# One chain for the first attention's modulation products, with loads a step ahead and a third raw slot; the samples' gate table loaded at the end of the attention's loop

## The chip, the cores and the metric

One core of a Trainium2 chip. The metric is device time in microseconds (us) of one execution of the whole program, the median of several runs. The engines: PE (TensorE, matmuls; PEld is its weight load), DVE (VectorE), ACT (ScalarE), POOL (GpSimd), and SP (SyncE), which issues every DMA of this kernel in one order, fixed when the program is built. Each engine, too, has one fixed order of instructions; an instruction that waits holds up all behind it on its engine.

## What is computed

One inference step of a two-layer encoder over 1024 prompt rows and 8 samples of 16 rows (1152 rows, width 1024). A layer is an attention and a convolutional MLP, each of this form:

```python
ada = (sc @ w_ada[l] + b_ada[l])[:, None, :]          # sc = silu(c), 9 rows: prompt + 8 samples
sh_m, sc_m, g_m, sh_f, sc_f, g_f = jnp.split(ada, 6, axis=-1)
h = x * (1 + sc_m) + sh_m
...
x = layer_norm(DEEPNORM_ALPHA * x + (1 + g_m) * mix, ln_g[l, 0], ln_b[l, 0])
```

Layer 0 attends to its own 64-row chunk and two before it, with 16 query heads, 4 key heads, a relative bias and sinks; layer 1 attends over 8 chunks back with keys and values of its own. The MLP is gelu-gated with a causal convolution of width 3.

## The kernel before

All arithmetic is float32 grade: every operand is split into a high and a low part (`split`: ACT casts the high part, L183, then DVE or POOL subtracts it, L194), and each product is three matmuls, low part of the weights first. A weight block of 512 KB is loaded into a raw slot of the ring `ws` (two slots), split into a slot of the ring `wring`, and then used (`wload`, L198).

The program opens with the first third of layer 0's modulation and the keys (`opening`), then `tables` and `attention(0)`. In the attention: keys' second half (L300), values (`vproj`, L326: nine tiles of 128 rows, the last three being 5, 6 and 7), then query block 0 (`qload(0)`, `qblock`, L313: 72 matmuls), whose weights go to the `wring` slot `w0r`. Then a loop over 64 pairs: scores (L558, L561), softmax (L525, L529), transposes (L587), values (L609), sums (L635), normalisation (L644, L647), the later query blocks, and from pair 24 on the 16 sample items (L701, L727, L736, L749). Values and keys go to DRAM and come back in another layout (kH, vH). On their way the eviction tiles are staged in X2 (named x2r) and, for what goes to the outputs, in six short tiles of the buffer F, at columns 9120, 9504, 10400, 11520, 11904 and 12288. Tile 7 of the values uses the one at 11520 and leaves from there to out_va (L388).

In the loop `self.step(BGA)` runs background work at 0.6 steps a pair: two generators `ada(1, 4)` and `ada(2, 4)`, the modulation groups 1 and 2. A step of `ada` loads one 512 KB block of w_ada into a raw slot (L232) and multiplies it by the conditioning rows (L240, 4 matmuls of 32 rows each, in the trace 8); after 16 steps one step loads the four bias pieces (L255) and adds them (L259), writes the gate table gd (L263, L265), and one transposes the result (L268). Groups 1 and 2 hold the gates of the attention and the scales and shifts of the MLP. While they run, score tiles have four PSUM banks; afterwards five.

Behind the loop, `out_proj` lays out F anew (`ln_region`), loads the prompt's gate row and the samples' gate table (`ln_gates`, L971 and L972) and the norm's rows behind the last normalisation's DMA, and then multiplies nine tiles of 128 rows (L326), the samples' tile first; L1122 multiplies a tile by its gates.

The order of the instructions is not that of the code: a scheduler places each by a model of the time in which it becomes ready, keeps what the data demand, and fixes the order of each engine. Matmuls of one modulation step are kept together by priorities (L232 ff.).

Of the kernel before, what the change touches and what calls it, by code (L numbers as in the profile page):

```python
# [10 lines left out]
F32 = mybir.dt.float32  # L11
# [4 lines left out]
D = 1024  # L16
# [89 lines left out]
class Trunk:  # L106
# [116 lines left out]
    def ada(self, gi, bank, ring=None):  # L223

        nc = self.nc
        ring = ring or self.ws
        ps = self.bank(bank)
        lead = [None] * 4
        for k in range(8):
            for hf in range(2):  # L230
                w = ring.next()
                nc.sync.dma_start(w, self.I["adaw"][gi, k, hf])  # L232
                for j in range(4):
                    with ExitStack() as es:
                        if lead[j] is not None:
                            es.enter_context(self.tc.issue_after(lead[j]))
                        if j:
                            es.enter_context(self.tc.high_priority())
                            es.enter_context(self.tc.issue_after(first))
                        mm = nc.tensor.matmul(  # L240
                            ps[32 * j : 32 * j + 32, hf * 256 : hf * 256 + 256],
                            self.cT[:, k * 32 : k * 32 + 32],
                            w[:, j * 256 : j * 256 + 256],
                            start=k == 0 and hf == 0,
                            stop=k == 7 and hf == 1,
                            tile_position=(0, 32 * j),
                            skip_group_check=True,
                        )
                    first = mm.ins if j == 0 else first
                    lead[j] = lead[j] or mm.ins  # L250
                yield
        row = ring.next()
        bsrc = self.I["adab"][gi : gi + 1, :]
        for j in range(4):
            nc.sync.dma_start(  # L255
                row[32 * j : 32 * j + 32, 512:1024].rearrange("p (h x) -> p h x", h=2),
                bass.AP(bsrc.tensor, bsrc.offset + j * 256, [[0, 32], [1024, 2], [1, 256]]),
            )
        nc.vector.tensor_add(row[:, 0:512], ps, row[:, 512:1024])  # L259
# [6 lines left out]
        yield  # L266
        for i in range(4):
            nc.tensor.transpose(ps[:, i * 128 : i * 128 + 128], row[:, i * 128 : i * 128 + 128], self.ident)  # L268
# [124 lines left out]
    def attention(self, l, wk):  # L393
        nc, I = self.nc, self.I
# [41 lines left out]
        assert fa.o <= self.NF, fa.o  # L436
        sbk = Ring(list(SB[l]))
        tbk = Ring(TB[l])
        obk = Ring(OB[l])
# [505 lines left out]
    def ln_region(self):  # L945
        fa = Arena(self.F)
        x = fa.take(2048)
        self.xring = Ring([x[:, i * 1024 : i * 1024 + 1024] for i in range(2)])
        y = Arena(x)
        self.yg = y.ring(2, 384)  # L950
        self.at = y.ring(2, 384)
        for k in ("hf", "xr", "tmp"):
            setattr(self, k, fa.take(1024))
        self.E = fa.take(704)
        self.cw = fa.take(176)
        self.uo = [fa.take(198) for _ in range(2)]
# [4 lines left out]
        self.zt = fa.take(1024)  # L961
        assert fa.o <= self.NF, fa.o

    def ln_consts(self, l, i):
        self.ln_gates(l, i)
        self.ln_rows(l, i)

    def ln_gates(self, l, i):
# [3 lines left out]
        nc.sync.dma_start(self.gateS, bass.AP(g.tensor, g.offset + D, [[D, 8], [0, 16], [1, D]]))  # L972

    def ln_rows(self, l, i):
        nc = self.nc
# [118 lines left out]
    def out_proj(self, l, xsrc, xdst, aff):  # L1094
        nc, I, H = self.nc, self.I, self.H
        w = [self.wo[i] if i in self.wo else self.woload(l, i) for i in range(8)]
        w0, w1 = w[0:4], w[4:8]
        self.wring = Ring(self.wslots[3:4] + self.wslots[0:3])
        self.ln_region()
        with self.tc.issue_after(self.lastdma):  # L1100
            self.ln_consts(l, 0)
        mb = Ring([0, 1, 2, 3])
        tb = Ring([4, 5, 6, 7])
        hfr = Ring([self.hf, self.zt])
        order = (8, 0, 1, 2, 3, 4, 5, 6, 7)
        acc = {}

        def half(t, hf):
            acc[t, hf] = self.bank(mb.next())
            self.mmX(acc[t, hf], t * 128, (w0, w1)[hf], 2, 512)  # L1110

        for t in order[:2]:
            half(t, 0)
        for t in order:
            if t not in order[:2]:
                half(t, 0)
            half(t, 1)
            x = self.residual(t, xsrc)
            gate = self.gateP if t < 8 else self.gateS
            for hf in range(2):  # L1120
                cs = slice(hf * 512, hf * 512 + 512)
                nc.vector.tensor_mul(self.tmp[:, cs], acc[t, hf], gate[:, cs])  # L1122
            nc.vector.scalar_tensor_tensor(x, x, ALPHA, self.tmp, op0=ALU.mult, op1=ALU.add)
            self.norm_tail(t, x, xdst, aff, False, tb, "a", "pv", Ring([self.xr]), hfr, hdst=self.hD)
# [812 lines left out]
    def build(self):  # L1937
        nc, I, O = self.nc, self.I, self.O
        self.bgrate = 0
        wk = self.opening()  # L1940
        self.bg = [self.ada(1, 4), self.ada(2, 4)]
        self.tables()
        self.attention(0, wk)
        self.drain()
        aff = self.affine(0, (3, 4), 0)
        self.out_proj(0, I["xrow"], self.xd[0], aff)
        self.ffn(0, self.xd[0], self.xd[1], lambda: self.affine(3, (6, 7), 1))
        self.attention(1, None)
        self.out_proj(1, self.xd[1], self.xd[2], self.affine(5, (11, 12), 2))
        self.ffn(1, self.xd[2], O["y"], lambda: None)  # L1950
# [131 lines left out]
```

## Time and profile before

| | us |
|---|---|
| median of 3 runs (2744.03 to 2745.9) | 2744.65 |
| profiled execution, whole | 2745.36 |
| profiled execution, span from first to last instruction | 2743.6 |
| mean granted clock of PE | 0.990 of full speed |
| first attention with opening and values | 0 to about 380 |
| output projection of layer 0 | about 380 to 460 |

The profile's page gives busy times of the engines over the span; further views list groups of instructions, waits (who waited for whom), the instructions in order of time, and busy times and clock by stretches. Times in them count from the span's start. The granted clock is the share of PE's full clock that its throttle let through.

### The profile page before, as it was taken

To read this page: it belongs to the slowest core of one execution; us is meant where nothing else is said; L and a number is where in the kernel's file an instruction comes from. 1 tells how busy PE (TensorE), PEld (TensorE's weight loads), DVE (VectorE), ACT (ScalarE), POOL (GpSimd) and SP (SyncE) were. 2 spreads that over 40 slices of the span, in tenths; PEclk is the share of its full clock that TensorE was granted. 3 is DMA by queue.
4 is the path that set the end of the run, shared out by engine and by line. 5 is a ranking of instruction groups with operands and counts; after the bars stand their busy time and mean duration, and the time that the engine had idled before them with its cause. 6 is when DMAs were issued, how large, how long until landed. Compare 5 with 4: busy or idle time off the path is not lost.

```text
span 2743.6 us, 47063 instructions
## 1 busy us (share of the span) xinstructions
PE 2639.7 (96%) x17266; PEld 2339.8 (85%) x17266; DVE 1936.4 (71%) x3840; ACT 1350.6 (49%) x2777; POOL 1069.0 (39%) x771
## 2 busy tenths in 40 slices
PE   7999889999999999999999999989989999999997
PEld 5997768989999998888898888867889999998886
DVE  4376768786676675767854667776888877778668
ACT  3475734443333344443536666573444455546553
POOL 2132523444443457665220121242367666652101
PEclk9999999999999999999999999999999999999999
DMA  8756534744444447666758546774444433349673
GB/s 298 234 155 199 152 104 169 239 155 140 140 150 148 153 144 231 238 207 203 261 196 264 146 136 182 207 232 134 160 149 171 150 134 138 123 140 301 222 236 123
DMA packets 229527, 498.27 MB, mean 182 GB/s; under 512 B 37456, under 2 KB 99232, under 8 KB 229296
## 3 DMA queue, kind: packets, MB, share of 16 engines
q1 hardware_dynamic: 229296, 495.27, 55.6%
q8 instruction: 136, 2.23, 0.3%
q14 instruction: 95, 0.78, 0.1%
HBM read 378.15 MB, written 126.47 MB: 184 GB/s over the span
## 4 chain that ended last, share of the span: by engine, by line
PE 38%; DVE 6%; DMA 3%; issue 1%; ACT 1%; POOL 1%; SPq 0%; DVEq 0%; POOLq 0%; ACTq 0%
PE PS L1237 14%; PE PS L1627 9%; PE PS L326 5%; PE PS L313 4%; PE PS L609 2%; PE PS L587 2%; DVE wl L194 1%; PE PS L558 1%; PE PS L561 1%; DVE F L525 1%; PE PS L736 1%; DVE xa L194 0%; DVE F L1197 0%; DMA F<-in_cvB_dram 0%; DVE PS L1286 0%
## 5 line engine op out<-in xcount | busy, mean ns | idle before, releaser
L1237 PE MATMUL PS<-H,wh 128*128 128x256 f32 (+1 forms) x2304 | 352.4, 294 | 0.0
L1237 PEld LDWEIGHTS PS<-H,wh 128*128 128x128 f32 x2304 | 319.8, 188 | 0.0
L1197 DVE TENSOR_TENSOR F<-PS,F 128x256 f32<-128x256 f32 (+1 forms) x446 | 196.9, 451 | 165.1 <-PE PS L1237 155.7
L183 ACT CAST wh<-F 128x512 fp32r<-128x512 f32 (+3 forms) x221 | 135.5, 625 | 196.8 <-PE PS L1237 96.2
L194 DVE TENSOR_TENSOR wl<-F,wh 128x512 fp32r<-128x512 f32 (+2 forms) x205 | 197.1, 972 | 44.1 <-ACT wh L183 40.6
L1237 PE MATMUL PS<-H,wl 128*128 128x320 f32 (+1 forms) x1152 | 202.3, 296 | 7.3 <-DVE wl L194 4.4
L1237 PEld LDWEIGHTS PS<-H,wl 128*128 128x128 f32 x1152 | 169.6, 189 | 13.7 <-issue 4.8
L1237 PE MATMUL PS<-xa,wh 128*128 128x320 f32 (+1 forms) x1168 | 179.8, 295 | 0.0
L1237 PEld LDWEIGHTS PS<-xa,wh 128*128 128x128 f32 x1168 | 163.1, 189 | 0.0
L1495 DVE TENSOR_TENSOR xa<-xa 128x384 fp32r<-128x384 f32 x66 | 99.1, 1515 | 81.0 <-ACT xa L183 80.9
L183 ACT CAST wh<-ws 128x512 fp32r<-128x512 f32 (+1 forms) x123 | 90.8, 744 | 119.3 <-PE PS L1237 50.3
L647 POOL TENSOR_TENSOR F<-F,x2r 64x512 f32<-64x512 f32 x62 | 79.3, 1279 | 165.8 <-DVE F L623 148.8
L1357 POOL TENSOR_TENSOR F<-F 128x1152 f32<-128x1152 f32 x44 | 124.7, 2834 | 44.3 <-DVE F L1350 24.0
L313 PE MATMUL PS<-H,w0r 128*128 128x384 f32 (+1 forms) x720 | 137.0, 341 | 0.3
L1286 DVE SCALAR_TENSOR_TENSOR F<-F 128x1024 f32<-128x1024 f32 (+2 forms) x160 | 132.4, 876 | 4.6 <-ACT F L1325 3.7
L326 PE MATMUL PS<-xa,H 128*128 128x512 f32 x504 | 128.9, 397 | 5.1 <-ACT xa L183 3.3
L313 PE MATMUL PS<-H,wh 128*128 128x384 f32 (+1 forms) x672 | 131.2, 339 | 0.0
L313 PEld LDWEIGHTS PS<-H,w0r 128*128 128x128 f32 x720 | 124.4, 188 | 2.8 <-issue 0.6
L525 DVE CUSTOM_DVE_ANT_0 F<-PS,F,C 128x256 f32<-128x256 f32 (+3 forms) x208 | 97.5, 480 | 40.6 <-PE PS L587 20.3
L587 PE MATMUL PS<-C,F 128*128 128x128 f32 x720 | 112.6, 281 | 13.3 <-DVE wh L594 5.9
L194 POOL TENSOR_TENSOR wl<-ws,wh 128x1024 fp32r<-128x1024 f32 x28 | 73.5, 2626 | 124.9 <-ACT wh L183 87.7
L326 PE MATMUL PS<-wh,H 128*128 128x512 f32 (+1 forms) x468 | 117.8, 360 | 0.5 <-ACT wh L183 0.5
(361 smaller groups left out, 6961.3 us busy)
## 6 DMA issues: line engine op xcount, KB each, us to landing
ws<-in_adaw_dram SPq DMA_DIRECT2D x63, 512.0 KB
ws<-in_wup_dram SPq DMA_DIRECT2D x51, 512.0 KB
F<-in_adaw_dram SPq DMA_DIRECT2D x49, 512.0 KB
actD<-F SPq DMA_DIRECT2D x33, 576.0 KB
F<-in_wup_dram SPq DMA_DIRECT2D x37, 512.0 KB
ws<-in_wdn_dram SPq DMA_DIRECT2D x33, 512.0 KB
F<-in_wdn_dram SPq DMA_DIRECT2D x33, 512.0 KB
xa<-kH SPq DMA_DIRECT2D x60, 256.0 KB
```

The lines of the kernel that those rows point to most:

```text
L183: nc.scalar.copy(out, in_)
L194: self.eng(el).tensor_sub(lo, src, hi.bitcast(F32))
L313: mm = self.nc.tensor.matmul(out[:, 0:n], w[a][:, k * 128 : k * 128 + 128], H[:, p, k, s0 : s0 + n], start=i == 0, stop=i == 23)
L326: self.nc.tensor.matmul(out[:, 0:n], H[:, p, j * kn + k, t0 : t0 + 128], w[a][:, k * n : k * n + n], start=i == 0, stop=i == 23,)
L525: nc.vector.tensor_tensor_reduce(out=p[:, c0 : c0 + w], in0=ps, in1=b, scale=1.0, scalar=init, op0=ALU.add, op1=ALU.min, accum_out=nm)
L587: nc.tensor.transpose(t[:, n * 128 : n * 128 + 128], p[:, (kt - k0) * 128 : (kt - k0) * 128 + 128], self.ident)
L1197: nc.vector.tensor_add(d, v(ps), a if len(a.shape) == 3 else v(a))
L1237: self.pairmm = nc.tensor.matmul(ps[:, 0:m], w[a][:, k * 128 : k * 128 + 128], x(p, k, n), start=start and c == 0, stop=c == 11, skip_grou ...
L1286: nc.vector.scalar_tensor_tensor(o, u, cw[:, cc, i : i + 1], o, op0=ALU.mult, op1=ALU.add)
L1357: nc.gpsimd.tensor_mul(yg, yg, ya)
L1495: nc.vector.tensor_sub(lo, raw, hi.bitcast(F32))
L1627: self.downmm = nc.tensor.matmul(ps, a[p][:, i * 128 : i * 128 + 128], w[q], start=first and c == 0, stop=last and c == 2, skip_group_chec ...
```

## The change

`ada_ahead` takes the place of the two generators: one chain of 34 records, 17 for each group (16 weight blocks, then the bias rows); each step first fetches the record of the next step into a raw slot and then works on the one fetched before. The ring of raw slots has a third slot in the first attention, `gateS`, at F columns 11644 to 12668; the value and query weights of that attention draw from the same ring. rb and the two sb tables move to X2 to make room. The samples' gate table has its own place now (that slot, or X2 in layer 1) and is loaded behind the attention's loop; zt takes its old place in F.

```diff
+    def ada_ahead(self, gis, bank):
+        nc, I = self.nc, self.I
+        ps = self.bank(bank)
+        def fetch(r):
+            gi, k = r
+            w = self.ws.next()
+            if k < 16:
+                nc.sync.dma_start(w, I["adaw"][gi, k // 2, k % 2])
+                return w
...
+        records = [(gi, k) for gi in gis for k in range(17)]
+        w = fetch(records[0])
         yield
+        lead = [None] * 4
+        for r, ahead in zip(records, records[1:] + [None]):
+            gi, k = r
+            now, w = w, fetch(ahead) if ahead else None
+            if k == 16:
+                self.ada_row(gi, ps, now)
+                yield
+                self.ada_turn(gi, ps, now)
...
-        rb = self.X2[:, 3840:4352].bitcast(F32)
+        rb = self.X2[:, 3072:3584].bitcast(F32)
+        self.gateS = self.X2[:, 3584:4608].bitcast(F32) if l else self.F[:, 11644:12668]
+        narrow = self.ws
+        if l == 0:
+            self.ws = Ring(narrow.items + [self.gateS])
...
-        sb = fa.ring(2, 272)
+        sb = fa.ring(2, 272) if l else Ring([self.X2[:, o : o + 272].bitcast(F32) for o in (3584, 3856)])
...
             if not self.bg and len(sbk.items) == 4:
                 sbk.items = [0, 1, 2, 3, 4]
+                self.ws = narrow
...
         assert not items
+        self.ws = narrow
+        g = self.gd[2 * l]
+        nc.sync.dma_start(self.gateS, bass.AP(g.tensor, g.offset + D, [[D, 8], [0, 16], [1, D]]))
...
+        self.zt = fa.take(1024)
-        for k in ("gateS", "gateP", "lng", "lnb"):
+        for k in ("gateP", "lng", "lnb"):
...
         with self.tc.issue_after(self.lastdma):
-            self.ln_consts(l, 0)
+            self.ln_gates(l, 0, False)
+            self.ln_rows(l, 0)
...
-        self.bg = [self.ada(1, 4), self.ada(2, 4)]
+        self.bg = [self.ada_ahead((1, 2), 4)]
```

Numbers of lines differ in the changed kernel: there L291 is the load of a modulation block, L323 its matmuls, L374 those of a query block, L387 those of the values, L444 and L449 the stores to vH and out_va, L553 and L554 the loads of keys and values, L904 the samples' gate table.

Three places in the built order follow; each row is a line, an operation, what it writes and reads, and the semaphores that it waits for.

SP, where the query weights (wq0) are loaded. Before, from row 38 of SP on, behind the caches' loads (ckA, cvA) and around the first key stores (kH):

```order
L674 DMA F_83<-in_ckA_dram 128x8x128 [waits DMAHW1_49,PE_49]
L676 DMA F_83<-in_cvA_dram 128x8x128 [waits DMAHW2_49,PE_49]
L1807 DMA ea_111<-F_83 16x384 [waits DMAHW3_49,DVE_49]
L198 DMA ws_79<-in_wq0_dram 128x1024 [waits DMAHW5_49,DMAHW4_49,Pool_49]
L351 DMA kH0_90<-x2r_82 128x2x384 [waits DVE_49]
L351 DMA kH0_90<-x2r_82 128x2x384 [waits DMAHW6_49,DVE_49]
L1827 DMA ska_113<-ea_111 2048x1x384 [waits DMAHW7_49,DMAHW3_49]
```

Now, from row 81 to row 90 (the block at row 41 is query weights 1 in the changed kernel):

```order
L444 DMA vH0_94<-x2r_82 128x512 [waits DMAHW4_49,DVE_49]
L449 DMA out_va_dram<-F_83 128x256 [waits DMAHW5_49,Activation_49]
L542 DMA x2r_82<-ska_113 32x1x144 [waits DMAHW6_49]
L542 DMA x2r_82<-ska_113 32x1x144 [waits DMAHW7_49]
L553 DMA wl_78<-kH0_90 64x1024 [waits DMAHW0_49]
L291 DMA ws_79<-in_adaw_dram 128x1024 [waits DMAHW1_49,PE_49]
L554 DMA xa_406<-vH0_94 128x8x128 [waits DMAHW4_49,DMAHW2_49]
L554 DMA xa_406<-vH0_94 128x8x128 [waits DMAHW3_49]
L198 DMA F_83<-in_wq0_dram 128x1024 [waits DMAHW5_49]
L291 DMA F_83<-in_adaw_dram 128x1024 [waits DMAHW4_49,Pool_49]
```

The load of query weights 0 has moved from row 41 to row 89, from a slot of ws to the third slot (F), behind the last value tile's two stores (rows 81 and 82), one block of the modulation (row 86) and the loads of the values (L554); it waits for the store to out_va (DMAHW5).

PE, at the passage from the values to query block 0. Before, from row 201:

```order
L326 MATMUL PS_89<-wh_77,H_75 128x256 x8
L326 MATMUL PS_89<-wl_78,H_75 128x256 x4
L326 MATMUL PS_89<-wh_77,H_75 128x256 x4
L313 MATMUL PS_89<-H_75,w0r_81 128x384 [waits DVE_49,Pool_49]
L313 MATMUL PS_89<-H_75,w0r_81 128x384 x23
L313 MATMUL PS_89<-H_75,w0r_81 128x384 [waits DVE_49]
L313 MATMUL PS_89<-H_75,w0r_81 128x384 x3
```

Now, from row 202:

```order
L387 MATMUL PS_89<-wl_78,H_75 128x256 x4
L387 MATMUL PS_89<-wh_77,H_75 128x256 x4
L323 MATMUL PS_89<-ws_79,C_84 32x256 [waits DMAHW2_49]
L323 MATMUL PS_89<-ws_79,C_84 32x256 x3
L374 MATMUL PS_89<-H_75,w0r_81 128x384 [waits Pool_49]
L374 MATMUL PS_89<-H_75,w0r_81 128x384 x7
L374 MATMUL PS_89<-H_75,w0r_81 128x384 [waits Activation_49]
L374 MATMUL PS_89<-H_75,w0r_81 128x384 x63
```

The first modulation step has moved ahead of query block 0; the 72 matmuls of that block stand in one piece and wait for POOL, which writes w0r, as before.

SP, at the attention's end, where the samples' gate table is loaded (the read of gd with three dimensions). Before, from row 273, among the last normalisation's transfers (rD) and the norm's rows (ln):

```order
L638 DMA rD0_100<-F_83 4x128 [waits DMAHW5_49,DVE_49]
L1258 DMA F_83<-in_sc_dram 128x704 [waits DMAHW6_49,DMAHW5_49,PE_49]
L644 DMA x2r_82<-rD0_100 64x512 [waits DMAHW2_49,Pool_49]
L971 DMA F_83<-gd_110 128x1024 [waits DMAHW0_49,PE_49]
L972 DMA F_83<-gd_110 128x1x1024
L979 DMA F_83<-in_ln_dram 128x1024 [waits PE_49]
```

Now, from row 255:

```order
L602 DMA F_83<-ska_113 128x256 [waits DMAHW2_49,DVE_49]
L724 DMA H_75<-oN_98 128x1024 [waits DMAHW4_49,DMAHW1_49]
L703 DMA rD0_100<-F_83 4x128 [waits DVE_49]
L904 DMA F_83<-gd_110 128x1x1024 [waits DMAHW5_49,Activation_49,Pool_49]
L709 DMA x2r_82<-rD0_100 64x512 [waits DMAHW6_49,DMAHW4_49]
L198 DMA ws_79<-in_wo0_dram 128x1024 [waits DMAHW7_49,Pool_49]
```

The table has moved from row 277 to row 258 of SP, ahead of the last stores and loads of the normalisation.

More of the change, by code (lines that the diff above doesn't have):

```diff
@@ L258, in ada, with ada_row @@
             )
+        self.ada_row(gi, ps, row)
+        yield
+        self.ada_turn(gi, ps, row)
+        yield
+    def ada_row(self, gi, ps, row):
+        nc = self.nc
         nc.vector.tensor_add(row[:, 0:512], ps, row[:, 512:1024])
@@ L265, in ada, with ada_turn @@
                 nc.sync.dma_start(self.gd[g, :, j * 256 : j * 256 + 256], row[32 * j : 32 * j + 9, 512:768])
-        yield
+    def ada_turn(self, gi, ps, row):
+        nc = self.nc
         for i in range(4):
@@ L272, in ada @@
             nc.vector.tensor_copy(dst[:, h], src[:, h, :, :, 0:9])
-        yield
+    def ada_ahead(self, gis, bank):
[7 more added lines that the diff above has]
+                return w
+            bsrc = I["adab"][gi : gi + 1, :]
+            for j in range(4):
+                nc.sync.dma_start(
+                    w[32 * j : 32 * j + 32, 512:1024].rearrange("p (h x) -> p h x", h=2),
+                    bass.AP(bsrc.tensor, bsrc.offset + j * 256, [[0, 32], [1024, 2], [1, 256]]),
+                )
+            return w
+        records = [(gi, k) for gi in gis for k in range(17)]
+        w = fetch(records[0])
+        yield
+        lead = [None] * 4
[4 more added lines that the diff above has]
+                self.ada_row(gi, ps, now)
+                yield
+                self.ada_turn(gi, ps, now)
+                lead = [None] * 4
+                yield
+                continue
+            hf = k % 2
+            for j in range(4):
+                with ExitStack() as es:
+                    if lead[j] is not None:
+                        es.enter_context(self.tc.issue_after(lead[j]))
+                    if j:
+                        es.enter_context(self.tc.high_priority())
+                        es.enter_context(self.tc.issue_after(first))
+                    mm = nc.tensor.matmul(
+                        ps[32 * j : 32 * j + 32, hf * 256 : hf * 256 + 256],
+                        self.cT[:, k // 2 * 32 : k // 2 * 32 + 32],
+                        now[:, j * 256 : j * 256 + 256],
+                        start=k == 0,
+                        stop=k == 15,
+                        tile_position=(0, 32 * j),
+                        skip_group_check=True,
+                    )
+                first = mm.ins if j == 0 else first
+                lead[j] = lead[j] or mm.ins
+            yield
     def affine(self, gi, v0, ln=None, e="p"):
@@ L435, in attention @@
         assert l == 0 or sa.o <= 720
-        assert fa.o <= self.NF, fa.o
+        assert fa.o <= (11644, self.NF)[l], fa.o
         sbk = Ring(list(SB[l]))
@@ L960, in ln_region, with ln_gates @@
         self.ya = Ring([y[:, i * 384 : i * 384 + 384] for i in range(3)])
-        self.zt = fa.take(1024)
         assert fa.o <= self.NF, fa.o
[L964 to L968, printed above, removed]
+    def ln_gates(self, l, i, samples=True):
         nc = self.nc
@@ L971, in ln_gates @@
         nc.sync.dma_start(self.gateP, bass.AP(g.tensor, g.offset, [[0, 128], [1, D]]))
-        nc.sync.dma_start(self.gateS, bass.AP(g.tensor, g.offset + D, [[D, 8], [0, 16], [1, D]]))
+        if samples:
+            nc.sync.dma_start(self.gateS, bass.AP(g.tensor, g.offset + D, [[D, 8], [0, 16], [1, D]]))
     def ln_rows(self, l, i):
```

## The prediction

> **What bounds the kernel.** The page is read first, then the waits of TensorE (PE) in the stretch of the change, then the order in time around them. A row of the waits names who waits for whom: us in total, times, longest.
>
> ```profile
> PE 2639.7 (96%) x17266; PEld 2339.8 (85%) x17266; DVE 1936.4 (71%) x3840; ACT 1350.6 (49%) x2777; POOL 1069.0 (39%) x771
> ...
> PE PS L240 <- DMA ws<-in_adaw_dram: 6.0, 5, 2.1
> PE PS L268 <- DVE ws L259: 1.9, 1, 1.9
> PE PS L326 <- DVE F L1122: 1.8, 1, 1.8
> ...
> PE PS L558 <- DVE F L525: 1.8, 5, 0.6
> ```
>
> PE is busy for 96% of the span, so the time is that of PE's program plus its waits. Between 70 and 480 us three waits belong to what the change touches: modulation matmuls on their loads (L240), the turn of the biased rows (L268), and the first gated tile of the output projection (L1122), whose releaser stands next.
>
> ```profile
> DVE F L1122 <- DMA F<-gd: 4.3, 1, 4.3
> ```
>
> That is the gate table. What the change may cost lies at the start of the attention, where PE does not wait at all (order in time: start, length, engine, line):
>
> ```profile
> 85.21 0.63 PE L326 MATMUL PS<-wh,H 128*128 128x256 f32 x4
> 85.68 12.88 PE L313 MATMUL PS<-H,w0r 128*128 128x384 f32 x72
> 98.40 1.40 PE L313 MATMUL PS<-H,wl 128*128 128x384 f32 x7
> ...
> 103.19 0.64 PE L240 MATMUL PS<-ws,C 128*32 128x256 f32 x8
> ```
>
> At 85.68 the last value tile (L326) is followed at once by the 72 matmuls of query block 0. They can, because their weights came long before:
>
> ```profile
> 56.51 0.35 SPq L198 DMA_DIRECT2D ws<-in_wq_dram  x1
> ...
> 60.73 1.05 ACT L183 CAST w0r<-ws 128x1024 fp32r<-128x1024 f32 x1 [1.49 <-DMA ws<-in_wq_dram]
> ...
> 61.86 2.41 POOL L194 TENSOR_TENSOR w0r<-ws,w0r 128x1024 fp32r<-128x1024 f32 x1 [2.70 <-ACT w0r L183]
> ```
>
> Load, cast and subtraction were over at 64.3, 21.4 us ahead of need.
>
> **What the change removes.** All 32 modulation loads are issued one step ahead into one slot more: I take the five waits at L240 as gone (their unrounded sum is 5.98). The bias rows come a step ahead: 1.92 at L268 goes. The gate table stands some twenty SP rows earlier: 1.81 at L326 goes. That is 9.7. What is late next: in the order the seventh weight block (k=6) reuses the third slot behind the split of query weights 2, with a cast and a 2.41 us subtraction before it, and the first turn follows its last product closely. I put back 1.5 for these two, about one wait of the old kind, and take **-8.2** (ends -9.7 and 0).
>
> The clock comes with it. Columns of the stretches: PE, PEld, DVE, ACT, POOL busy, granted clock, DMA share, GB/s.
>
> ```profile
> 222.90:231.00 8.10, 6.18 (x47) 4.17 (x47) 4.24 (x15) 3.41 (x11) 2.41 (x4) 0.79 0.83 279
> 317.00:326.00 9.00, 7.38 (x51) 5.66 (x51) 5.48 (x23) 4.95 (x13) 8.79 (x9) 0.62 0.57 158
> 387.00:394.00 7.00, 5.19 (x16) 3.86 (x15) 5.52 (x9) 2.14 (x2) 1.03 (x1) 0.76 0.53 193
> 120.00:126.00 6.00, 3.87 (x37) 2.63 (x37) 4.72 (x16) 4.88 (x16) 1.26 (x1) 1.00 0.77 221
> ```
>
> Three of the removed waits (ending at 224.8, 318.6 and 389.2) are followed by a lowered clock: 8.1 x 0.21 = 1.70, 9 x 0.38 = 3.42 and 7 x 0.24 = 1.68 us, 6.8 in all; the one ending at 124.5 is not. I count the first and the last as won and leave the middle one, which lies among other thin stretches: **-3.4** (ends -6.8 and 0).
>
> The Trainium skill, "TensorE: Matmul & The Clock Gate", Part 1 (the HAM clock gate), says that the array falls to half rate after an idle window of about 3.4 us and regains full rate after as long a busy one. By it waits below 2 us would cost no clock, and this term would be 0, the sum 3.4 higher. Here the trace disagrees: 0.79, 0.62 and 0.76 stand behind waits of 1.8 to 1.9 us.
>
> **What it adds: query weights 0 come late.** The third raw slot is the third entry of the ring, so the first load that takes it is the one of query weights 0, and it lies over F columns where the value projection's last tile is staged. So that load waits for the store of that tile (out_va), and in the order it stands at SP row 89 instead of 41, behind every load and store of the start. PE's order now has the first modulation step, then the 72 matmuls, which wait for POOL's half of the split (the low part is multiplied first). When is row 89 reached? SP's order in time before:
>
> ```profile
> 75.28 0.34 SPq L232 DMA_DIRECT2D ws<-in_adaw_dram  x1
> ...
> 96.48 0.53 SPq L383 DMA_DIRECT2D vH<-x2r  x1
> 97.32 0.34 SPq L388 DMA_DIRECT2D out_va_dram<-F  x1
> 102.70 1.00 SPq L489 DMA_DIRECT2D xa<-vH  x2
> 103.89 1.70 SPq L232 DMA_DIRECT2D ws<-in_adaw_dram  x2
> ...
> SPq L489 <- DMA vH<-x2r: 5.0, 2, 3.4
> ...
> 86.74 0.37 ACT L387 COPY F<-PS 128x256 f32<-128x256 f32 x1 [0.49 <-DVE x2r L382]
> ```
>
> Rows 54 to 88 ran here from 75.28 to 103.70. The same 35 transfers, in another order, stand at rows 54 to 88 now, so without more, row 89 is issued at 103.9. The last tile's data were ready at 87.1 and their store still went at 96.48: SP was backed up. That store stands four rows earlier now (81, not 85), 2.7 us at the pace of this stretch (33 rows in 22.4 us), with less in the rings ahead of it; so its landing, for which row 87 waits, comes at about 99, and behind the two value loads the query load goes at **about 100.1**. Ahead of it in the rings lie the step's weight block and two value loads of 512 KB each. Before, two value and two weight loads went from 102.70 to 105.6:
>
> ```profile
> 96.00:100.00 4.00, 4.00 (x25) 4.00 (x24) 1.11 (x3) 1.41 (x4) 0.59 (x4) 1.00 1.12 234
> 100.00:104.00 4.00, 4.00 (x29) 3.33 (x29) 1.46 (x6) 1.96 (x6) 0.00 (x0) 1.00 0.45 138
> 104.00:108.00 4.00, 4.00 (x33) 3.41 (x33) 3.90 (x15) 3.08 (x11) 0.00 (x0) 1.00 1.03 288
> 108.00:112.00 4.00, 4.00 (x27) 3.90 (x25) 1.38 (x7) 2.10 (x10) 0.00 (x0) 1.00 0.58 229
> ```
>
> These four (2.1 MB) moved in 104 to 112 (1.15 + 0.92 MB), done by about 110.3, 7.6 us after the first was issued. The four now, with the first value load at 99.1, land at about **106.7**. Bounds: a lone load took 3.2 us (next rows), and one in the most crowded stretch, issued at 64.62, let its cast start only at 76.50, 11.9 us later.
>
> ```profile
> 121.33 0.36 SPq L232 DMA_DIRECT2D ws<-in_adaw_dram  x1
> ...
> 124.52 0.64 PE L240 MATMUL PS<-ws,C 128*32 128x256 f32 x8 [2.13 <-DMA ws<-in_adaw_dram]
> ...
> 64.62 1.44 SPq L198 DMA_DIRECT2D ws<-in_wq_dram  x1
> ...
> 76.50 1.05 ACT L183 CAST wh<-ws 128x1024 fp32r<-128x1024 f32 x1 [1.53 <-DMA ws<-in_wq_dram]
> ```
>
> The Trainium skill, "DMA: Bandwidth & Descriptors", section on the anatomy of one DMA, has a fit of about 2.0 us and the bytes over 436 GB/s, an estimate of 3.2 us for 512 KB; it agrees with the lone load, and by it the load would land at 103.3 and the sum would be 3.4 lower, because it knows no queue ahead.
>
> Then 1.05 cast and 2.41 subtraction with 0.3 of hand-overs: PE starts block 0 at 106.7 + 3.8 = 110.5. It would have started at 85.68 plus the 0.6 of the step now ahead of it, 86.3: **+24.2**, all of it idle PE. Ends: with SP not backed up at all, 34 rows from 75.28 at their own issue times (some 19 us by the order in time) reach the load at 94.6, lone landing, start 101.6: +15.3; issued at 103.9 and landing 11.9 later, start 119.6: +33.3. Queued behind: on PE the whole attention, since its order is fixed; on ACT and DVE the evictions of block 0; on SP the second weight block, which waits for POOL's split, and query weights 2, which wait for that block's matmuls. All of these follow PE, and nothing is caught up: PE was busy without a gap in the four stretches above, so no wait there can absorb it.
>
> A pause this long leaves a low clock behind it; I take the row 387 to 394 as its price, **+1.7** (ends 0 and 3.4, the row 317 to 326).
>
> **What costs nothing.** The rb and sb tables move within on-chip memory. The eight sb loads now wait for two value stores, but their first reader, the first sample item, is far away:
>
> ```profile
> 178.40 0.41 PE L701 MATMUL PS<-F 128*32 128x144 f32 x2
> ```
>
> Some 80 us cover them; without these the item would wait for one landing, 3.2. The chain has one step more, so the fifth score bank opens two pairs later, at the loop's end; bounds 0 and one short wait of the scores, 0.6, and I take 0. The table and zt change places in F, and in the second layer the table is loaded earlier; no PE wait there is on either, so 0 both ways.
>
> **Sum.** 2745.36 (the profiled execution: span 2743.6 and 1.76 around it) + 24.2 + 1.7 - 8.2 - 3.4 = 2759.7, that is +14.3. Against the median 2744.65, which lies 0.7 lower: **2759.0**.
>
> **Rivals.**
> 1. *The queue is not backed up (not slower).* The load is issued at 94.6 and lands alone, the start costs 15.3 + 1.7; with all waits and clock won (-16.5) it ends at +0.5, 2745. For it: SP's rows cost 19 us of issue alone and DMA was half idle at 100 to 104. Against it: the 1.12 share at 96 to 100 and the 5.0 us wait for the store. It decides where the load is issued before about 95 (with the gains of the sum) or 100 and landing alone (with all gains). Only ahead of that, a start before 95.5, would it be faster.
> 2. *The load meets a full queue:* landing at 115.8, +33.3 + 1.7 - 11.6 = +23.4, 2768; with half the gains 2774.
> 3. *The change does not do what it says:* the loads a step ahead still wait, since SP works in order and stands behind query weights 2. Only L268 and the gate table are won (3.7, with 1.7 of clock): +20.5, 2765.
>
> **How the numbers follow.** Forecast 72% (2754 to 2768); rival 1 16%, of which 12 within 5.5 us and 4 faster; rival 2 8%; rival 3 4%. A measurement of this kernel tells 0.2% (5.5 us) from no change. So slower 0.84, same 0.12, faster 0.04. The range takes the forecast, rival 3 and the lower half of rival 2, and rival 1 only where it touches: **2750 to 2770**.
>
> **What would show it.** Right: an idle PE of 20 to 30 us ending at the first L374 matmul, released by POOL, with the query load issued at about 100; L323 without waits on its load, the turn and the first gated tile without theirs; from 130 on each stage some 25 us later, shrinking to some 14 by 420. Wrong: block 0 starts before 100, or the idle is there but a later stretch takes it back.

## The result, and the profile after

The changed kernel takes 2777.51 us (median of 4 runs, 2776.59 to 2784.67) against 2745.28 us: 1.0116 of the time before, 95% interval 1.0100 to 1.0132. In a second job it was 1.0112 (1.0098 to 1.0127). The direction was forecast, the size was not: +32 us for a forecast of +14, outside the range.

The page's busy times, and the waits of PE between 60 and 520 us (who waits for whom: us in total, times, longest):

```profile
PE 2646.8 (95%) x17266; PEld 2345.0 (84%) x17266; DVE 1941.3 (70%) x3840; ACT 1347.9 (49%) x2777; POOL 1070.1 (39%) x771
...
PE PS L374 <- POOL w0r L194: 24.4, 1, 24.4
PE PS L801 <- DVE F L688: 3.0, 2, 2.1
PE PS L323 <- DMA ws<-in_adaw_dram: 2.3, 3, 1.2
PE PS L652 <- DVE F L794: 1.6, 1, 1.6
...
PE PS L652 <- DVE F L701: 1.4, 1, 1.4
```

Where the page before had a modulation wait of 6.0 us on top there is one wait of 24.4 us, at the place that the prediction named. The three waits that were to go are gone or smaller (modulation loads 2.5 with the 0.2 on slot F, the biased rows and the first gated tile nothing), and two kinds that were small stand in the list: the sample items' matmuls (L801) and the transposes (L652), both waiting for DVE, 7.6 us together. In the two other profiles of this order (c_after and e3 below) they are 3.2 and 3.3 us, so part of that belongs to this execution.

The order in time around the pause, on SP, ACT, POOL and PE (start, length, engine, line):

```profile
95.40 0.35 SPq L449 DMA_DIRECT2D out_va_dram<-F  x1
...
99.00 1.01 SPq L554 DMA_DIRECT2D xa<-vH  x2
100.06 2.87 SPq L198 DMA_DIRECT2D F<-in_wq_dram  x1
...
107.92 1.05 ACT L183 CAST w0r<-F 128x1024 fp32r<-128x1024 f32 x1 [20.08 <-DMA F<-in_wq_dram]
...
109.10 2.34 POOL L194 TENSOR_TENSOR w0r<-F,w0r 128x1024 fp32r<-128x1024 f32 x1 [25.89 <-ACT w0r L183]
...
86.50 0.64 PE L323 MATMUL PS<-ws,C 128*32 128x256 f32 x8
111.50 14.15 PE L374 MATMUL PS<-H,w0r 128*128 128x384 f32 x72 [24.35 <-POOL w0r L194]
```

The load of query weights 0 is issued at 100.06 behind the last value tile's store and the value loads, its cast starts at 107.92, and PE starts block 0 at 111.50. Block 0 itself takes 14.15 us, not 12.88, at a granted clock of 0.90: the low clock behind the pause.

Now the rest. The stretch from the end of block 0 to the output projection's first product that reads x2r, in both profiles (length, then busy time of PE, PEld, DVE, ACT, POOL, granted clock, DMA share, GB/s), and the matmuls ahead of and behind the first gated tile:

```profile
98.56:385.36 286.80, 265.78 (x2105) 220.24 (x2104) 191.79 (x650) 182.55 (x518) 92.99 (x88) 0.98 0.53 161
...
125.65:420.23 294.58, 272.39 (x2096) 224.79 (x2096) 194.89 (x651) 182.29 (x518) 93.60 (x88) 0.95 0.49 150
...
392.88 0.89 PE L326 MATMUL PS<-wh,H 128*128 128x512 f32 x2
...
422.05 1.55 PE L387 MATMUL PS<-w0r,H 128*128 128x512 f32 x6
...
424.36 0.62 PE L387 MATMUL PS<-wh,H 128*128 128x512 f32 x2
```

The stretch is 7.8 us longer, not shorter. The sum of PE's waits in it went from 20.0 to 21.5; the rest of the difference is a longer busy time (272.39 for 265.78 us) for no more matmuls (one modulation step fewer, the one that went ahead of block 0), at a granted clock of 0.95 instead of 0.98. From these rows the 32.4 us between the two spans are put together so:

| part of PE's program | measured, us | as predicted, us |
|---|---|---|
| to the end of the values (85.68, now 86.50) | +0.8 | 0 |
| step ahead and pause (86.50 to 111.50) | +25.0 | +24.2 |
| low clock in block 0 (12.88, now 14.15) | +1.3 | +1.7 |
| loop up to the output projection (286.80, now 294.58) | **+7.8** | **-8.1** |
| first gated tile and its clock (385.36 to 392.88, now 420.23 to 424.36) | -3.4 | -3.5 |
| all behind it (to 2743.6, now 2776.0) | +0.9 | 0 |
| sum | +32.4 | +14.3 |

One row carries the miss. The second row holds 0.6 us of the step that moved ahead, which is missing from the loop; the pause itself is 24.35 against 24.2, and the loop, like for like, +8.4.

### The profile page after: what moved, and what is told of

Same layout as the page of the kernel before. It is cut to its first block, busy times and chain, and to the rows that moved or that the text cites. A ratio compares the mean times of both kernels' runs of the same rounds, so it can differ in the third digit from the quotient of the medians.

```text
span 2776.0 us, 47069 instructions
## 1 busy us (share of the span) xinstructions
PE 2646.8 (95%) x17266; PEld 2345.0 (84%) x17266; DVE 1941.3 (70%) x3840; ACT 1347.9 (49%) x2777; POOL 1070.1 (39%) x771
## 4 chain that ended last, share of the span: by engine, by line
PE 37%; DVE 6%; DMA 3%; ACT 2%; issue 1%; POOL 1%; SPq 0%; DVEq 0%; ACTq 0%; POOLq 0%
PE PS L1304 16%; PE PS L1694 9%; PE PS L387 4%; PE PS L374 3%; PE PS L674 2%; PE PS L652 2%; DVE wl L194 1%; PE PS L623 1%; DMA F<-hmD 1%; PE PS L626 1%; ACT F L1007 1%; DVE F L590 1%; PE PS L801 1%; DVE xa L194 1%; DMA F<-in_cvB_dram 0%
## 5 line engine op out<-in xcount | busy, mean ns | idle before, releaser
L1304 PEld LDWEIGHTS PS<-H,wh 128*128 128x128 f32 x2304 | 319.8, 188 | 0.0
L374 PE MATMUL PS<-H,w0r 128*128 128x384 f32 (+1 forms) x720 | 138.1, 343 | 24.4 <-POOL w0r L194 24.4
L374 PEld LDWEIGHTS PS<-H,w0r 128*128 128x128 f32 x720 | 125.5, 190 | 27.3 <-POOL w0r L194 24.8
L387 PE MATMUL PS<-xa,H 128*128 128x512 f32 x504 | 130.8, 400 | 5.1 <-ACT xa L183 3.3
L374 PE MATMUL PS<-H,wh 128*128 128x384 f32 (+1 forms) x672 | 131.2, 339 | 0.0
L652 PE MATMUL PS<-C,F 128*128 128x128 f32 x720 | 113.7, 282 | 16.6 <-DVE wh L659 5.9
L387 PE MATMUL PS<-wh,H 128*128 128x512 f32 (+1 forms) x468 | 117.1, 358 | 0.5 <-ACT wh L183 0.5
L387 PEld LDWEIGHTS PS<-xa,H 128*128 128x128 f32 x504 | 94.6, 191 | 27.1 <-ACT xa L183 3.8
L374 PEld LDWEIGHTS PS<-H,wh 128*128 128x128 f32 x672 | 116.9, 188 | 0.6 <-issue 0.4
```

The lines of the kernel that those rows point to most:

```text
L374: mm = self.nc.tensor.matmul(out[:, 0:n], w[a][:, k * 128 : k * 128 + 128], H[:, p, k, s0 : s0 + n], start=i == 0, stop=i == 23)
L387: self.nc.tensor.matmul(out[:, 0:n], H[:, p, j * kn + k, t0 : t0 + 128], w[a][:, k * n : k * n + n], start=i == 0, stop=i == 23,)
L652: nc.tensor.transpose(t[:, n * 128 : n * 128 + 128], p[:, (kt - k0) * 128 : (kt - k0) * 128 + 128], self.ident)
L1304: self.pairmm = nc.tensor.matmul(ps[:, 0:m], w[a][:, k * 128 : k * 128 + 128], x(p, k, n), start=start and c == 0, stop=c == 11, skip_grou ...
```

## The experiments

Every ratio below is to the kernel before in the same job. Jobs differ: the median of before was 2749.18, 2747.68, 2749.52 and 2747.90 us.

**Is the late load the main cost?** e1 gives query weights 0 a narrow slot again, e2 moves the staging tiles off the third slot instead:

```diff
 e1_q0_narrow
-        if l == 0:
-            self.ws = Ring(narrow.items + [self.gateS])
...
         qload(0)
+        if l == 0:
+            self.ws = Ring([narrow.items[1], self.gateS, narrow.items[0]])

 e2_tiles_moved
-        late = (9120, 9504, 11520, 11904, 12288, 10400)
+        late = (9120, 9504, 9888, 10784, 11168, 10400)
```

> The changed kernel, but query weights 0 go to a slot of the narrow ring as before (their load stands at SP row 41), and the third slot joins the ring behind them. Theory A, the late load of query weights 0 is the main cost and the first attention's loop lost some 7.5 us more of its own through the new order: the pause of 24.4 us ahead of query block 0 is gone, the loop still takes about 249 us, and the time is about 2750 us. Theory B, the loop's loss is an aftermath of the pause (low clock, transfers shifted against each other): the pause and the loop's loss are both gone, the gains of the loads a step ahead show, about 2737 us. Rival C, another transfer would have held PE at the same place anyway: a pause of over 10 us stays, 2765 us or more.

> The changed kernel, but the three staging tiles of F that lie under the third slot are moved to columns 9888, 10784 and 11168; query weights 0 still go to the third slot. If the overlap of slot and staging tile is what holds the load (theory A or B), it is issued near 50 us and there is no pause: about 2750 us (A) or 2737 us (B). If the place in the ring or a full DMA queue holds it, the pause of 15 us or more stays and the time is 2768 us or more.

e1: 2753.96 us, 1.0013 (1.0004 to 1.0023). e2: 2754.11 us, 1.0022 (1.0009 to 1.0035). The pause is gone in both, so the overlap of slot and staging tile holds the load, not its place in the ring as such, and it costs about 1.0116 - 1.0013, some 28 us (two jobs). Neither kernel shows the forecast gain, which is nearer to theory A. Both have a smaller cost of their own at the start, seen in PE's order in time (e1, then e2) and, in e1, SP's:

```profile
109.06 1.08 PE L323 MATMUL PS<-F,C 128*32 128x256 f32 x8 [4.87 <-DMA F<-in_adaw_dram]
...
102.27 8.29 SPq L291 DMA_DIRECT2D F<-in_adaw_dram  x2
...
94.35 9.04 PE L374 MATMUL PS<-H,w0r 128*128 128x384 f32 x41 [1.80 <-ACT F L448]
```

In e1 the first modulation block inherits the slot and the wait behind the store: 4.87 us. In e2 the query load is issued at 36.5 us, between the two blocks of value weights, and the values' eviction is late.

**Can that remainder be removed?** e7 lets the second modulation block, not the first, take the slot; e6 joins e1 and e2.

```diff
 e7_ring_turned, on e1
-            self.ws = Ring([narrow.items[1], self.gateS, narrow.items[0]])
+            self.ws = Ring([narrow.items[1], narrow.items[0], self.gateS])
 e6_q0_and_tiles, on e1
-        late = (9120, 9504, 11520, 11904, 12288, 10400)
+        late = (9120, 9504, 9888, 10784, 11168, 10400)
```

> As e1_q0_narrow, with the third slot last in the new ring, so that the second modulation block, not the first, takes it. In e1 the first product on that slot waited 4.87 us for its load (issued at 102.3, behind the last value tile's store). If that slot's first load is the remaining cost of the overlap: no wait over 2 us at the modulation products, and 4 to 5 us less than e1, ratio 0.9985 to 1.000. Rival: the wait passes to the second block, ratio as e1, 1.001 to 1.002.

> As e1_q0_narrow, with the staging tiles also moved off the slot: nothing of the overlap is left. Its first modulation block is then loaded at SP row 35, between the two blocks of value weights. If the overlap is all that is left: 4 to 5 us less than e1, ratio 0.9985 to 1.000. If the load between the value weights makes the values late (rival): a wait of 1 to 4 us ahead of the values or of query block 0, ratio 1.001 to 1.002.

No. e7: 2752.87 us, 1.0020 (1.0009 to 1.0031), and the wait has passed to the second block (4.48 us), as the rival said. e6: 2757.65 us, 1.0033 (1.0020 to 1.0046), again the rival, though dearer than the 1.001 to 1.002 that it gave: ACT's order in time shows the values' eviction waiting for the stores ahead of it, and block 0 then waits for ACT (the row of PE).

```profile
90.55 0.37 ACT L442 CAST x2r<-PS 128x256 fp32r<-128x256 f32 x1 [5.10 <-DMA vH<-x2r]
...
95.82 10.20 PE L374 MATMUL PS<-H,w0r 128*128 128x384 f32 x41 [3.26 <-ACT F L448]
```

**The late load alone, and the parts alone.** e8 has two raw slots and the old generators, with one load through the third slot's columns; e4 only the early gate table (and the moved tables); e5 the chain on two slots; e3 the three slots with the old generators.

```diff
 e4_gate_only, on the changed kernel
-            self.ws = Ring(narrow.items + [self.gateS])
...
-        self.bg = [self.ada_ahead((1, 2), 4)]
+        self.bg = [self.ada(1, 4), self.ada(2, 4)]
 e8_late_only, on e4
+            self.ws = Ring(narrow.items, [self.gateS])
         qload(0)
 e5_chain_two, on the changed kernel
-            self.ws = Ring(narrow.items + [self.gateS])
 e3_no_chain, on the changed kernel
-        self.bg = [self.ada_ahead((1, 2), 4)]
+        self.bg = [self.ada(1, 4), self.ada(2, 4)]
```

> Two raw slots and the old generators, only query weights 0 alone go once to the columns of the third slot. If the late load is nearly the whole of the change's cost: a pause of 24 to 25 us ahead of query block 0, a low clock behind it worth 1 to 2 us, and the loop as in the kernel before, 285 to 290 us: ratio 1.009 to 1.011. Rival: the pause costs less than its length since the transfers of the attention gain a lead behind it (fewer waits in the loop): 1.006 to 1.008.

> Neither chain nor third slot in the ring: of the change only the samples' gate table at the loop's end, with the moved rb and sb tables. If the gate table is worth its wait and the low clock behind it: 1.8 + 1.4 us, about 2742 us, and the first gated tile waits for nothing. Rival: the wait goes to another operand of that tile, 2745 us.

> The chain of loads a step ahead, but with two raw slots, and the early gate table. If loading ahead is worth the waits of the modulation matmuls (6.0 us) and of the biased rows (1.9 us) with their clock: 2742 minus 6 to 11, about 2734 us. If two slots leave no room to load ahead (each load still waits for the product or split that frees its slot): waits at the modulation matmuls as before, 2742 us, or more where the query weights now find their slot taken.

> The changed kernel with the two old generators in the chain's place, on three raw slots. Its built order is the changed kernel's, row for row on every engine. So the chain by itself does nothing, and the third slot everything: pause 24 to 25 us, ratio 1.010 to 1.013. Rival: the chain has a part that the order does not show; then the ratio leaves that interval.

e8: 2783.58 us, 1.0132 (1.0116 to 1.0147), more than either theory gave. The pause stands in PE's order in time in pieces, since five modulation steps (L240) were put ahead of block 0, one in the changed kernel. It ends where block 0 starts, at 112.88 (111.50 in the changed kernel):

```profile
103.05 1.08 PE L240 MATMUL PS<-ws,C 128*32 128x256 f32 x8 [15.24 <-DMA ws<-in_adaw_dram]
...
111.75 1.08 PE L240 MATMUL PS<-ws,C 128*32 128x256 f32 x8 [6.26 <-DMA ws<-in_adaw_dram]
112.88 13.95 PE L374 MATMUL PS<-H,w0r 128*128 128x384 f32 x72
```

So a kernel with nothing else of the chain or the slot loses as much as the whole change. Its loop took 295.3 us, not the 285 to 290 expected; its later order differs from e4's too, so the excess over 28 us isn't the load's for certain. e4: 2750.98 us, 1.0001 (0.9988 to 1.0014, that is -3.3 to +3.8 us): the wait of the gated tile is gone from the profile and no time can be measured for it. e5: 2757.26 us, 1.0033 (1.0019 to 1.0047); with two slots a block fetched ahead is written over before it is multiplied, so its modulation differs, at equal work. Its modulation waits were not less but more (7.5 us on the blocks, 2.7 on the bias rows): two slots leave no room. e3: 2775.86 us, 1.0101 (1.0088 to 1.0114), in the interval: its pause is 24.1 us. With three slots the scheduler puts the same loads and products in the same places whether the code fetches a step ahead or not. **With three slots the chain by itself does nothing; the third slot makes the new order.** (With two slots it does something, for the worse: e5.)

**How steady is the loop?** The two kernels again, as controls.

> The kernel before, unchanged, as a second profile of one built order. In the profile before, PE was busy 264.7 us from the first score (99.64) to the output projection's second weight split (385.36); in e4_gate_only, whose PE order is the same, 270.5 us. Theory V (the clock's share differs from one execution to the next by more than the loop's loss of the changed kernel): the stretch here has 264 to 272 us busy at a granted clock of 0.95 to 0.98, and waits near 20 us. Rival: 264.7 us within 1 us, and then the 6 to 8 us more in the other kernels are theirs.

> The changed kernel again, in one job with the others. Pause of 24 to 25 us ahead of query block 0, issued near 100 us as before; time 1.010 to 1.013 of the kernel before. Were the pause chance (a crowded queue in one execution), its length here would differ by more than 5 us.

c_before: 2748.15 us, 1.0001 (0.9992 to 1.0010). c_after: 2777.83 us, 1.0112, pause 24.9 us: it is no chance of one execution. The stretch of the loop, for c_before, c_after and e3, which has the changed kernel's order:

```profile
99.32:386.06 286.74, 268.57 (x2106) 222.72 (x2104) 191.78 (x650) 182.56 (x518) 93.03 (x88) 0.97 0.52 160
...
127.25:420.62 293.37, 273.10 (x2096) 223.70 (x2096) 194.83 (x651) 182.51 (x519) 93.82 (x88) 0.95 0.50 152
...
125.68:413.44 287.76, 269.10 (x2096) 221.80 (x2096) 193.33 (x651) 182.41 (x518) 92.94 (x88) 0.97 0.50 154
```

The order before took 286.8 and 286.7 us; the new one 294.6, 293.4 and 287.8. So with one order 6.8 us of this stretch belong to the execution (or to the chip: the jobs ran on different ones), by waits and clock together, and of the +7.8 of a single pair of profiles only about 1 is in every pair. In e4, with the PE order of before, the stretch took 296.5 us in a run of 2752.98 us, while the runs of that kernel go from 2742.96 to 2757.55; but the orders of SP and DVE differ there, so its 9.8 us more isn't the execution's alone. That no profile with three slots came near the 278.7 us that the prediction implied stands all the same.

One reading of these profiles says more than the sum. DVE copies a row of reciprocal sums out of PSUM 32 times in this attention (L636 before, L701 in the changed kernel); the 25th copy cuts the loop ahead of the output projection's first products. Times are in us; waits and busy times are PE's:

| | before | c_before | after | c_after | e3 |
|---|---|---|---|---|---|
| end of block 0 to the 25th copy | 208.6 | 205.6 | 205.0 | 204.4 | 203.5 |
| from there to the end of the stretch | 78.2 | 81.2 | 89.6 | 88.9 | 84.3 |
| waits in this last part | 13.8 | 12.4 | 16.8 | 13.6 | 13.1 |
| busy in this last part | 64.0 | 68.3 | 72.5 | 74.7 | 70.8 |
| granted clock in this last part | 0.96 | 0.89 | 0.87 | 0.85 | 0.90 |
| waits of the modulation, whole stretch | 7.9 | 5.4 | 2.5 | 3.4 | 2.4 |
| all waits, whole stretch | 20.0 | 16.8 | 21.5 | 19.2 | 17.7 |

The new order is ahead up to the 25th copy and loses more than that in the last part, in every pair. The modulation's waits are won, yet on the mean the sum of all waits is no smaller (18.4 before, 19.5 now), and the larger part of the loss is busy time. Some 15 matmuls more fall into the last part (504 records for 489), and its granted clock is lower in two of the three profiles than in either before. How much each of these two has is not shown.

**Where does the gain of the loads go?** e9 sends the output weights through the narrow slots. e11 is the clean case: two slots until pair 9, then three, so that the start pays nothing.

```diff
 e9_wo_narrow, on e1
+                held, self.ws = self.ws, narrow
                 self.woload(l, WAT[i])
+                self.ws = held
 e11_joins_later, on e4
+        two = list(narrow.items)
...
+            if l == 0 and i == 9:
+                k = narrow.i % 2
+                narrow.items, narrow.i = [self.gateS, two[k], two[1 - k]], 0
...
```

> As e1_q0_narrow, but the output projection's weights loaded in the loop come through the two narrow slots. The six kernels with three slots had 12 to 14 us of low clock in the last 110 us ahead of the output projection, the two profiles before 5 and 10. If the earlier output weights, whose splits then fall among the sample items, cause that: 5 to 9 us of low clock here and ratio 1.000. If the modulation's products, now ahead of the sample items and missing between them, cause it: as e1, 1.001 to 1.002.

> Two raw slots up to pair 9, then three; the two old generators (with three slots the chain builds the same order), the early gate table. No load on the start's path uses the third slot, and no product waits for it at the start, so this is the third slot's worth in the loop alone. If the slot is worth the waits at the modulation's loads (6.0 us) and their clock: ratio 0.997 to 0.999 and waits of the loop 4 to 8 us below e4_gate_only. If the loop gives them back among the sample items: those waits gone, others in their place, ratio 1.000 to 1.002.

e9: 2751.23 us, 1.0014 (1.0002 to 1.0026), as e1; here too a raw block is written over before its use, so part of the modulation differs, at equal work. The low clock in the last 110 us was worth 8.5 us (summed over stretches of 10 us; by the same sum 11.9 in e1, 3.4 and 8.5 in the two profiles before), within the 5 to 9 of the first theory, yet the time stayed e1's, as the second had it: the output weights are not what takes the gain, and the clock of one profile does not decide the time. e11: 2750.02 us, 1.0008 (0.9994 to 1.0021). **No gain of the third slot can be measured in the loop** even without a cost at the start; the interval leaves it 1.6 us at most. Its profile shows one place where the won waits went: PE's waits, DVE's and SP's rows behind the second one, and the stretch that follows:

```profile
PE PS L240 <- DMA ws<-in_adaw_dram: 3.4, 6, 0.8
PE PS L650 <- DVE F L699: 3.3, 1, 3.3
...
306.75 3.05 SPq L701 DMA_DIRECT2D rD<-F  x1
...
317.20 0.28 DVE L699 COPY F<-PS 4x128 f32<-4x128 f32 x1 [3.31 <-DMA rD<-F]
...
317.53 1.11 PE L650 MATMUL PS<-C,F 128*128 128x128 f32 x4 [3.32 <-DVE F L699]
...
310.00:330.00 20.00, 14.65 (x99) 10.34 (x98) 11.26 (x43) 14.48 (x38) 13.65 (x11) 0.64 0.68 189
```

The modulation's waits fell from 7.0 us (e4) to 3.4. But the row of reciprocal sums has one buffer: DVE may copy the next only when the last store of 2 KB to rD is done, and that store now stands on SP behind five loads of the outputs (512 KB each), the gate table and a cache block, and is issued over 3.05 us. PE, further on than in e4 (the 25th copy came 6.2 us earlier in the stretch), waits 3.3 us for it; then the clock is at 0.64 for 20 us. From the 25th copy to the 28th e11 took 34.7 us, the two profiles before 26.6 and 27.6. In the changed kernel the same copy (L701) waits 1.4 us for the same store, and PE behind it 1.4; PE's wait there is 0.4 in c_after and in e3, so this is the account of e11 and only a part of that of the changed kernel. Nor is it e11's whole account: its waits in the loop are 19.5 us for e4's 24.0, as the first theory had it (4 to 8 less), and the two loops still took the same 296.5 us, e11's at a clock of 0.94 and e4's at 0.96.

**Which of the three won waits was real?** e10 keeps two slots and the old generators and uses the free columns for the bias rows alone, loaded half a group ahead; e12 is e10 without the early gate table.

```diff
 e10_rows_early, on e4
+                if row is not None and k == 4 and hf == 0:
+                    self.ada_bias(gi, row)
                 w = ring.next()
...
-        self.bg = [self.ada(1, 4), self.ada(2, 4)]
+        self.bg = [self.ada(1, 4, row=self.F[:, 11644:12668]), self.ada(2, 4, row=self.F[:, 11644:12668])]
 e12_rows_only, on e10: the gate table is loaded where it was before
```

> Two raw slots, old generators, the early gate table as in e4_gate_only, and the bias rows loaded half a group ahead into the columns of the third slot, which the ring does not use here. If the waits off the modulation's turn can be won without the third slot's cost: no wait at the turn, the time below e4_gate_only and the kernel before by 1.9 us of wait and 1 to 3 of clock, ratio 0.998 to 0.9995. Rival: the time comes back in the sample items, ratio 1.000 to 1.001.

> e10_rows_early without the early gate table: its built order differs in four rows of SP alone. If e10's gain is that of the bias rows: ratio 0.996 to 0.998, and the first gated tile waits some 2 us again. If the early gate table has a part in it: 0.998 to 1.000.

e10: 2739.51 us (2734.95 to 2741.39), **0.9963 (0.9952 to 0.9975)**. e12: 2742.40 us, 0.9977 (0.9965 to 0.9990). Both beat the kernel before and the changed one. The turn of the biased rows waits for nothing, as expected. That the gated tile would wait again in e12 was wrong: its table lands in time. e10's advantage over e12 lies within the intervals. In e12's profile the span is 5.8 us shorter than before's: the loop 0.7 (286.10), the first gated tile 3.4, the part behind it 2.8, and the start 1.1 longer. So the gain is measured, but what brings it is not shown: the turn's wait is gone, yet the loop in which it stood has only 0.7 of the 5.8. A rival is untested: the bias rows no longer take a raw slot, and the waits of the weight blocks are lower too (4.3 us in e10 and 3.6 in e12, for 6.0 and 4.4 in the two profiles before).

## Why the prediction was wrong

**The late load (+24.2, measured +24.4, or 25.0 with the step ahead of it) and its clock (+1.7, measured +1.3): right.** The order of SP, the pace at which it was backed up and the queue ahead of the load gave an issue at about 100.1 and a start of PE at 110.5; they were 100.06 and 111.50. The fit of the Trainium skill, "DMA: Bandwidth & Descriptors", section on the anatomy of one DMA, whose estimate was a landing at 103.3, was too early by over 4 us here: the cast that waits for the load began at 107.92. (The page gives that fit for DMAs issued by GpSimd; these are issued by SP.) e1 and e2 show the cause by taking the overlap away, e8 by making it alone.

**The gains in the loop (-8.1): this is the step that failed.** It was put as "I take the five waits at L240 as gone", the bias rows' 1.92 as gone, and half of the clock behind them as won. The waits did go (L240's 6.0 us became 2.5, the turn's 1.9 nothing), but the time did not come: PE's waits in the stretch are 20.0 us before and 21.5 after, and the loop is 7.8 us longer, 1.0 to 7.8 over the three profiles of the new order. What failed is the step from a wait that goes to a time that is won. The prediction asked what is late next only of the loads and the turn themselves (the 1.5 that it put back), not of the rest of the loop. There the lead lasts to the 25th copy; behind it other waits come (in e11 the normalisation's store behind its loads, in the changed kernel waits for DVE's work, at the sample items above all), and PE is busy for longer. e11 has the loop without the start's cost: 1.0008 (0.9994 to 1.0021), a gain of 1.6 us at most, where the prediction had 8.1. The clock's -1.7 failed with it: the loop's granted clock was 0.98 and 0.97 before and 0.95, 0.95 and 0.97 after. The forecast sign "from 130 on each stage some 25 us later, shrinking to some 14" began to come true, 23.5 at the 25th copy, and then turned: 34.9 at the end of the stretch.

**The first gated tile (-3.5, measured -3.4): right in its place, but no gain of the program is shown,** for e4 alone came to 1.0001 (0.9988 to 1.0014).

**What costs nothing:** held; the sb loads and the tables left no wait of their own.

**The rivals.** 1 fell: the queue was backed up. 2 fell too, although its 2768 to 2774 lies nearest to the time: the load did not meet a fuller queue. 3 fell in its form (the modulation's loads wait less), but its head, that the change does not do what it says, is true of the chain, as e3 shows.

**What stays open.** How much of the loop's +7.8 is the order's and how much the execution's: one built order gave 287.8 to 294.6 us. And why PE is busy longer in the last part of the loop: no run separates the matmuls that moved there from the lower clock. The timed kernels bound it: with three slots and no pause they lie 0.1 to 0.3% above the kernel before, of which e1, e2, e6 and e7 have 2 to 5 us of waits at the start.

## What to carry to other kernels

A buffer joined to a ring brings to every user of that ring the dependences of the memory it lies on: look up which transfer takes the new slot first, and what must leave it before. A removed wait counts only after the next one on the way has been looked for, to the end of the loop and not at the same place alone; in e11 the next was one store of 2 KB away. And where a scheduler orders by readiness, writing loads ahead in the code can change nothing that one slot more does not change alone, as it was here.

## What the runs showed of the hardware

Equal waits do not always lower the clock. At the start of the output projection both kernels have the same two waits, and only the changed one then has a slow piece (before, then after):

```profile
364.91 1.21 PE L326 MATMUL PS<-xa,H 128*128 128x512 f32 x4 [1.46 <-DVE xa L194]
...
367.43 3.02 PE L326 MATMUL PS<-xa,H 128*128 128x512 f32 x12
...
396.61 1.22 PE L387 MATMUL PS<-xa,H 128*128 128x512 f32 x4 [1.47 <-DVE xa L194]
...
399.81 5.19 PE L387 MATMUL PS<-xa,H 128*128 128x512 f32 x12
```

Twelve equal matmuls took 3.02 and 5.19 us, at granted clocks of 1.00 and 0.55; ahead of the two waits (355 to 362.71, and 390 to 394.41) the clock was 1.00 in both. A price for the clock behind a wait, read from one profile, can therefore be wrong by its whole size.

A subtraction of 128x1024 on DVE took 1.21 us in the profile before and 2.66 in the one after, with POOL busy beside it in both (DVE's order in time); the second holds up the sample items' copies behind it, and PE waits 1.64 us for those.

```profile
338.45 1.21 DVE L194 TENSOR_TENSOR xa<-ws,xa 128x1024 fp32r<-128x1024 f32 x1
...
363.36 2.66 DVE L194 TENSOR_TENSOR xa<-ws,xa 128x1024 fp32r<-128x1024 f32 x1
```
